# Softmax sums on GpSimd, attention's loads on the sync queue: an encoder block on one Trainium2 core

## The chip, the cores and the metric

The kernel runs on one core of a Trainium2 chip. A core has TensorE (PE, matmuls into PSUM), VectorE (DVE) and ScalarE (ACT), which read and write SBUF and PSUM, GpSimd (POOL), and the sync engine (SP), which here only issues transfers. Each engine works through its own instructions in order and waits on semaphores for the others. The metric is the device time of one execution in microseconds (us).

## The reference

One layer of a hybrid encoder on 2048 tokens of width 1024 and 16 meta tokens ahead of them. The input projection gives queries (4 heads of 128), keys and values (2 groups) and a Fourier part; attention and the Fourier part are normalized apart and projected back, then comes a feed-forward part of width 4096.

```python
proj = hn @ w_in[i]
q = axial_rope(rms_norm(q, g_q[i]), cos_r, sin_r, cos_c, sin_c)
k = axial_rope(rms_norm(k, g_k[i]), cos_r, sin_r, cos_c, sin_c)
attn = block_attention(q, k, v)
four = fourier_mix(u, w_fourier[i])
mixed = jnp.concatenate([rms_norm(attn, g_attn_out[i]), rms_norm(four, g_fourier_out[i])], axis=-1)
h = h + mixed @ w_out[i]
m = rms_norm(h, g_mlp[i])
h = h + jnp.square(jax.nn.relu(m @ w_up[i])) @ w_down[i]
...
s = jnp.einsum('bkgqd,bksd->bkgqs', qb, kt).astype(jnp.float32) * scale
p = jax.nn.softmax(s, axis=-1).astype(vt.dtype)
return jnp.einsum('bkgqs,bksd->bkgqd', p, vt)
```

## The kernel before

The kernel runs in stages: the input projection with norms and rotations (it stores queries, keys and values in DRAM, `q_d`, `k_d`, `v_n`, `v_m`); the U pass (`u_pass`), the Fourier transforms (`fourier`) and their output projection (`out_f`); attention's output projection (`out_a`); then up and down products of the feed-forward part. Most products are made of three matmuls of rounded parts (`mm3`, L81 to L83).

Attention (`attention`, L782) has no stage of its own. It is a generator of 16 units; a unit is 256 queries of one group of two heads (512 columns) against all keys, in 17 steps: 16 blocks of 128 keys and one of the meta tokens. `mix` (L1065) calls it so many steps for each step of the stage that it runs beside; the steps in the U pass, in the Fourier transforms, in `out_f` and in `out_a` are fixed by numbers (`ULEAD`, `FLEAD`, `OLEAD`, `STEPS_A`). So each engine's order is a weave of attention and the other stage. Where the code doesn't tie two instructions (`tc.issue_after`), a list scheduler chooses the order in which an engine's instructions stand.

`scores` (L812) makes one block's scores `s` on TensorE; ScalarE copies them to the pair's tile `S` (two blocks, 128 x 1024, L833), and VectorE keeps the running maximum `M` (L836, L839). `S` has 11 buffers (`S_BUFS`). At a unit's end `stats` (L859) turns the maximum into `mb` through TensorE, VectorE and ScalarE. `softmax` (L866) runs 17 + 3 steps behind the scores (`LEADT`): for each pair VectorE subtracts `mb` (L893), ScalarE takes the exponential in place (L894), VectorE adds the pair to `acc` (L898 for the first add, L900 for the other six), and TensorE multiplies by the values into `o` (L902). At the unit's end the two halves of `acc` are added (`sum`, L880), and `finish` (L904) divides.

Keys (`kt`, `load_k`), values (`vn`, `load_v`) and queries (`q`, `load_q`) are loaded on GpSimd's queue. GpSimd has little else in this part: the power -1/2 of each norm (`rstd_of`, L194: `rs_f` for the Fourier rows, `rs_a` and `rs_m` in `out_a`), sums of squares (L1018) and the loads of the Fourier tables (L608, L611). The sync queue loads and stores the rest, such as the residual rows `xo` (L1003) and `h_d`, and the attention output `o_d`.

Of the kernel before, what the change touches and what calls it, by code (L numbers as in the profile page):

```python
# [14 lines left out]
ALU = mybir.AluOpType  # L15
# [16 lines left out]
NT = SEQ // P  # L32
HALF = L // 2
QUART = HALF // 2
REM = 96
MR = 96
# [21 lines left out]
def f32v(ap):  # L58
    return ap.bitcast(F32)
# [26 lines left out]
def ins_of(x):  # L86
    return getattr(x, "ins", x)
# [49 lines left out]
def encoder_block(ctx: ExitStack, tc: tile.TileContext, x, meta, w_in, w_f,  # L137
                  w_out, w_up, w_down, g_fin, g_cols, g_rows, c_id, c_rope, c_dft, c_even, c_odd, c_rem, out):
    nc = tc.nc
# [21 lines left out]
    tp = Lines(tc.alloc_tile_pool(name="p1", bufs=2, side="right"), small)  # L161
# [20 lines left out]
    mhalf = const.tile([P, 8], F32, name="mhalf", tag="mhalf")  # L182
# [3 lines left out]
    c_ao = lambda k: cols[:, 16 + k:17 + k]  # L186
    c_fo = lambda k: cols[:, 20 + k:21 + k]

    def rstd_of(pool, ss, n, width, tag, rows=P):

        ms = pool.tile([P, n], F32, name="ms_" + tag, tag="ms_" + tag, bufs=2 if pool is tp else 4)
        nc.vector.tensor_scalar(ms[:rows], ss, 1.0 / width, EPS, op0=ALU.mult, op1=ALU.add)
        rs = pool.tile([P, n], F32, name="rs_" + tag, tag="rs_" + tag, bufs=2 if pool is tp else 4)
        nc.gpsimd.tensor_tensor(rs[:rows], ms[:rows], mhalf[:rows, :n], op=ALU.pow)  # L194
        return rs

    q_d = [dram.tile([P, 2, NQ, 256], F32, name=f"q_d{b}") for b in range(8)]
    k_d = dram.tile([P, NKV, 2, SEQ + MR], F32, name="k_d")
    v_n = dram.tile([P, NKV, NT, P], F32, name="v_n")
    v_m = dram.tile([MR, NKV, P], F32, name="v_m")  # L200
# [395 lines left out]
    def load_tables(tr):  # L596

        src, full, rest, n_tab = sources(tr)
        rem = ft.tile([P, NG, REM], F32, name=f"rem{tr}", tag="rem", bufs=1)
        nc.vector.memset(rem, 0.0)  # L600
        for o in (0, 32, 64):
            for lo, hi in rest:
                nc.vector.tensor_copy(rem[:, :, o:o + hi - lo], src[:, :, lo:hi])
                o += hi - lo
        tabs = []
        for nt in range(n_tab):
            t = ft.tile([P, 4, CHP], R32, name=f"tab{tr}_{nt}", tag="tab", bufs=T_BUFS)[:, :, :CH]
            nc.gpsimd.dma_start(t, c_even[tr, nt] if tr < 2 else c_odd[tr - 2, nt])  # L608
            tabs.append((t[:, 0:2], t[:, 2:4]))
        t = ft.tile([P, 2, CHP], R32, name=f"tabr{tr}", tag="tabr", bufs=2)[:, :, :CH]  # L610
        nc.gpsimd.dma_start(t[:REM], c_rem[tr])  # L611
        tabs.append(t)
        tables[tr] = tabs, rem

# [92 lines left out]
    def fourier():  # L707
        for par in range(2):
            pc = transform(2 * par)
            yield  # L710
            C = {}
            for g in range(NG):
                for c in range(2):
                    ps = pc(g, c)
                    C[g, c] = fp.pool.tile([P, CHP], F32, name=f"C{par}_{g}_{c}", tag="C", bufs=8)[:, :CH]
                    nc.scalar.copy(C[g, c], ps)
                yield
            sn = transform(2 * par + 1)
            yield
            for g in range(NG):  # L720
                for c in range(2):
                    ps = sn(g, c)
                    i0, step = (c * CH, 1) if par else (1 + c, 2)
                    m0 = -(min(i0 - 8, 0) // step)
                    e0, e1 = i0 + step * m0 - 8, i0 + step * (CH - 1) - 8
                    (t, col, _, n), = y_runs(par, e0, e1 + 1)
                    nc.vector.tensor_tensor(t[:, g, col:col + n:step], C[g, c][:, m0:], ps[:, m0:], op=ALU.subtract)
                    m1 = CH - 1 if (par == 0 and c == 1) else CH
                    e1 = SEQ // 2 - par - i0
                    e0 = e1 - step * (m1 - 1)  # L730
                    (t, col, _, n), = y_runs(par, e0, e1 + 1)
                    nc.vector.tensor_tensor(t[:, g, col:col + n:step][:, ::-1], C[g, c][:, :m1], ps[:, :m1], op=ALU.add)
                yield
# [14 lines left out]
    KC = 4 * P  # L748
    KCP = 640

    def load_k(u, g, c):
        n = KC + (MR if c == 3 else 0)
        kt = ap.tile([P, 2, KCP if c == 3 else KC], R32, name=f"kt_{u}_{c}", tag=f"KT{c // 3}", bufs=1 if c == 3 else 3)
        nc.gpsimd.dma_start(kt[:, :, :n], k_d[:, g, :, c * KC:c * KC + n])
        return kt

    def load_v(u, g, c):
        if c == 4:
            vt = ap.tile([P, P], R32, name=f"vm_{u}", tag="VM", bufs=1)
            nc.gpsimd.dma_start(vt[:MR], v_m[:, g])  # L760
        else:
            vt = ap.tile([P, 4, P], F32, name=f"vn_{u}_{c}", tag="VT", bufs=4)
            nc.gpsimd.dma_start(vt, v_n[:, g, 4 * c:4 * c + 4])
        return vt

    o_d = [dram.tile([P, 2, NQ, 512], F32, name=f"o_d{b}") for b in range(4)]
# [10 lines left out]
                    nc.sync.dma_start(f32v(A[:, e, k]), o_d[b][:, e, k])  # L777
        return AT[b]

    held = {}  # L780

    def attention():  # L782

        units = [(b0 + qh, g) for i, (b0, n) in enumerate(BLOCKS)
# [3 lines left out]
        def load_q(u):  # L788
            b, g = units[u]
            q = ap.tile([P, 2, 2, 256], R32, name=f"q_{u}", tag="q", bufs=2)  # L790
            nc.gpsimd.dma_start(q, q_d[b][:, :, 2 * g:2 * g + 2])
            return q.rearrange("p l h n -> p l (h n)")

        def start(u, q=None):
# [71 lines left out]
        def softmax(u, i):  # L866

            s = state[u]
            nm = f"{u}_{i}"
            vt = KV["v", u]  # L870
            if i == NT:
                S = s["S"][-1][:MR]
# [11 lines left out]
            j = i // 2  # L884
# [5 lines left out]
            p = S  # L890
            if i % 2 == 0:
                mb = s["mb"].rearrange("p (o n) -> p o n", o=1).broadcast_to([P, 2, 512])
                nc.vector.tensor_tensor(S, S, mb, op=ALU.subtract)  # L893
                held["exp"] = ins_of(nc.scalar.activation(p, S, AF.Exp, scale=ISQ))  # L894
                return
            v = vt[j // 2]
            if j == 1:
                nc.vector.tensor_tensor(acc, s["S"][0], p, op=ALU.add)  # L898
            elif j > 0:
                held["sub"] = ins_of(nc.vector.tensor_tensor(acc, acc, p, op=ALU.add))  # L900
            for e in range(2):
                nc.tensor.matmul(s["O"], v[:, 2 * j % 4 + e], p[:, e], start=i + e == 1, stop=False)  # L902

# [94 lines left out]
    def out_f():  # L998
# [6 lines left out]
        def rows(t):  # L1005

            hi = op_.tile([P, NG, P], R32, name=f"yh_{t}", tag="yh", bufs=2)
            lo = op_.tile([P, NG, P], R32, name=f"yl_{t}", tag="yl", bufs=2)
            sq = op_.tile([P, NG, P], F32, name=f"ysq_{t}", tag="ysq", bufs=2)
            for par in range(2):  # L1010
                for src, col, e, n in y_runs(par, 64 * t, 64 * t + 64):
                    y = src[:, :, col:col + n]
                    o = 2 * (e - 64 * t) + par
                    v = slice(o, o + 2 * n - 1, 2)
                    split(hi[:, :, v], lo[:, :, v], y)
                    nc.scalar.square(sq[:, :, v], y)
            for n in (2, 1):
                nc.gpsimd.tensor_tensor(sq[:, :n], sq[:, :n], sq[:, n:2 * n], op=ALU.add)  # L1018
            ops[t] = [hi, lo, sq]

        def scale(t):
# [820 lines left out]
```

## Time and profile before

| | us |
|---|---|
| runs, median (lowest to highest) | 2239.28 (2238.01 to 2241.07) |
| the profiled execution | 2236.94 |
| its span | 2235.2 |
| softmax adds on VectorE: L898, 16 of 1217 ns, and L900, 96 of 1219 ns | 19.5 and 117.0 |
| subtractions on VectorE, L893, 128 of 1222 ns | 153.0 |
| tensor instructions on GpSimd in attention's stages: sums of squares, L1018, 16 of 1293 ns and 16 of 1095 ns | 20.7 and 17.5 |

The profile is of one execution. Busy time is the time in which an engine worked on an instruction of the program; it says nothing on whether anything waited for it. Matmuls are pipelined, so that their rows overlap; the time from one start to the next is what one costs. A group's row gives the shape, the count, the busy time, the mean of one, and the idle time of the engine ahead of them with what ended it.

### The profile page before, as it was taken

The numbers are of one execution on the slowest core, as the hardware profiler recorded it, in microseconds if no ns is written. First come the engines' busy times: TensorE is split into PE (matmuls) and PEld (weight loads), VectorE is DVE, ScalarE is ACT, GpSimd is POOL, SyncE is SP. The second block draws the span as 40 slices with busy tenths as digits, with TensorE's granted clock in tenths as the row PEclk, the third lists the DMA queues.
The fourth block names the chain that finished last, engine by engine and source line by source line (L and its number), as shares of the span: only waits on it lengthen the run. The fifth ranks groups of instructions, "written<-read, shape, count | busy, mean of one in ns | idle before, by whom it ended". The sixth has DMA issues, their size and how long they took to land.

```text
span 2235.2 us, 27654 instructions
## 1 busy us (share of the span) xinstructions
PE 2219.0 (99%) x9890; PEld 1752.8 (78%) x9890; DVE 1681.4 (75%) x2260; ACT 1170.8 (52%) x1991; POOL 255.8 (11%) x301
## 2 busy tenths in 40 slices
PE   9999999999999999999999999999999999999998
PEld 7888867777777666677888888888888888888887
DVE  6566299999888989887676778679656555796795
ACT  6554255655554667677555654334455555443243
POOL 2223101012132212110000020000100000200000
PEclk9999999999999999999999999999999999999999
DMA  7685743345346434476767585434594434955442
GB/s 244 207 264 175 255 134 90 88 114 166 118 146 206 160 95 139 133 266 231 264 225 243 198 296 192 164 125 151 213 360 151 163 138 164 344 169 160 134 130 85
DMA packets 219914, 408.08 MB, mean 183 GB/s; under 512 B 19568, under 2 KB 97776, under 8 KB 218112
## 3 DMA queue, kind: packets, MB, share of 16 engines
q1 hardware_dynamic: 192000, 343.64, 45.9%
q0 software_dynamic: 27632, 62.41, 9.1%
q8 instruction: 78, 1.28, 0.2%
q14 instruction: 60, 0.49, 0.1%
q10 hardware_dynamic: 144, 0.26, 0.0%
HBM read 260.16 MB, written 146.08 MB: 182 GB/s over the span
## 4 chain that ended last, share of the span: by engine, by line
PE 45%; DVE 3%; DMA 3%; ACT 1%; issue 1%; SPq 0%; POOLq 0%; POOL 0%; DVEq 0%; ACTq 0%
PE dx L81 5%; PE dx L83 5%; PE dx L82 5%; PE dy L81 4%; PE dy L83 4%; PE dy L82 4%; PE ux L83 3%; PE ux L82 3%; PE ux L81 3%; PE uy L81 3%; PE uy L83 3%; PE uy L82 3%; DMA f_d<-lf 2%; DMA lf<-m_d 1%; DVE wul L72 1%
## 5 line engine op out<-in xcount | busy, mean ns | idle before, releaser
L71 ACT CAST ah<-a 128x1024 fp32r<-128x1024 f32 x108 | 113.0, 1050 | 263.7 <-PE dx L82 107.2
L902 PE MATMUL o<-S,vn 128*128 128x512 f32 x512 | 242.8, 595 | 0.0
L833 ACT COPY S<-s 128x512 f32<-128x512 f32 x256 | 147.8, 587 | 143.4 <-PE s L83 136.8
L83 PE MATMUL dx<-bh,al 128*128 128x512 f32 x496 | 192.5, 388 | 0.0
L82 PE MATMUL dx<-bl,ah 128*128 128x512 f32 x496 | 192.5, 388 | 0.0
L81 PE MATMUL dx<-bh,ah 128*128 128x512 f32 x496 | 192.5, 388 | 0.0
L83 PE MATMUL ux<-bf,wul 128*128 128x512 f32 x448 | 174.3, 389 | 0.7 <-DVE wul L72 0.7
L81 PE MATMUL ux<-bf,wuh 128*128 128x512 f32 x448 | 174.6, 390 | 0.0
L82 PE MATMUL ux<-bf,wuh 128*128 128x512 f32 x448 | 174.3, 389 | 0.0
L893 DVE TENSOR_TENSOR S<-S,mb 128x1024 f32<-128x1024 f32 x128 | 153.0, 1222 | 17.6 <-ACT mb L864 17.6
L894 ACT ACTIVATE S<-S 128x1024 f32<-128x1024 f32 x128 | 134.5, 1065 | 50.0 <-DVE S L893 48.8
L72 DVE TENSOR_TENSOR al<-a,ah 128x1024 fp32r<-128x1024 f32 x108 | 131.3, 1221 | 31.7 <-ACT ah L71 31.3
L81 PE MATMUL s<-q,kt 128*128 128x512 f32 (+1 forms) x272 | 151.0, 555 | 1.8 <-DMA kt<-k_d 1.0
L81 PE MATMUL dy<-bh,ah 128*128 128x512 f32 (+1 forms) x388 | 150.5, 388 | 0.0
L82 PE MATMUL dy<-bl,ah 128*128 128x512 f32 (+1 forms) x388 | 150.5, 388 | 0.0
L83 PE MATMUL dy<-bh,al 128*128 128x512 f32 (+1 forms) x388 | 150.5, 388 | 0.0
L902 PEld LDWEIGHTS o<-S,vn 128*128 128x128 f32 x512 | 93.3, 189 | 69.1 <-issue 58.5
L81 PE MATMUL uy<-bf,wuh 128*128 128x512 f32 x320 | 124.9, 390 | 1.2 <-ACT wuh L71 1.2
L82 PE MATMUL uy<-bf,wuh 128*128 128x512 f32 x320 | 124.8, 390 | 0.0
L83 PE MATMUL uy<-bf,wul 128*128 128x512 f32 x320 | 124.7, 390 | 0.0
L1306 ACT ACTIVATE c<-c 128x512 f32<-128x512 f32 x96 | 60.5, 631 | 121.4 <-DVE c L1354 117.8
L839 DVE TENSOR_TENSOR M<-M,S 128x1024 f32<-128x1024 f32 x96 | 117.8, 1227 | 7.3 <-ACT S L833 6.1
(330 smaller groups left out, 5576.5 us busy)
## 6 DMA issues: line engine op xcount, KB each, us to landing
a<-s_d SPq DMA_DIRECT2D x84, 512.0 KB, 3.8
R<-in_w_up_dram SPq DMA_DIRECT2D x32, 1024.0 KB, 5.5
s_d<-s SPq DMA_DIRECT2D x128, 256.0 KB, 2.1
s_d<-c SPq DMA_DIRECT2D x96, 256.0 KB, 2.7
d<-in_w_down_dram SPq DMA_DIRECT2D x48, 512.0 KB, 5.1
f_d<-lf SPq DMA_DIRECT2D x56, 256.0 KB, 3.1
bf<-f_d SPq DMA_DIRECT2D x7, 2048.0 KB, 13.8
hk<-ht_d SPq DMA_DIRECT2D x24, 512.0 KB, 4.8
```

What stands on the lines that cost most here:

```text
L71: self.high = nc.scalar.copy(hi, src)
L72: self.low = nc.vector.tensor_tensor(lo, src, f32v(hi), op=ALU.subtract)
L81: nc.tensor.matmul(out, a[0], b[0], start=first, stop=False, skip_group_check=chain)
L82: nc.tensor.matmul(out, a[0], b[1], start=False, stop=False, skip_group_check=chain)
L83: nc.tensor.matmul(out, a[1], b[0], start=False, stop=last, skip_group_check=chain)
L833: nc.scalar.copy(S[:, i % 2], ps)
L839: nc.vector.tensor_tensor(M, M, S, op=ALU.max)
L893: nc.vector.tensor_tensor(S, S, mb, op=ALU.subtract)
L894: held["exp"] = ins_of(nc.scalar.activation(p, S, AF.Exp, scale=ISQ))
L902: nc.tensor.matmul(s["O"], v[:, 2 * j % 4 + e], p[:, e], start=i + e == 1, stop=False)
L1306: nc.scalar.activation(dst, src, AF.Relu)
```

## The change

Six of a unit's seven adds to `acc` are issued on GpSimd; the last, with pair 7, stays on VectorE (now L908). A helper, `on_pool`, ties GpSimd's instructions from the adds, the norms of all but the first stage, the sums of squares, the Fourier tables and the meta values in program order. Keys, values and queries are loaded by the sync queue. The tables of transform 2 are loaded one step earlier, ahead of the products of transform 1.

```diff
+    held = {}
+
+    def on_pool(call, *args, **kw):
+
+        with tc.issue_after(held["pool"]) if "pool" in held else nullcontext():
+            held["pool"] = ins_of(call(*args, **kw))
...
-        nc.gpsimd.tensor_tensor(rs[:rows], ms[:rows], mhalf[:rows, :n], op=ALU.pow)
+        if pool is tp:
+            nc.gpsimd.tensor_tensor(rs[:rows], ms[:rows], mhalf[:rows, :n], op=ALU.pow)
+        else:
+            on_pool(nc.gpsimd.tensor_tensor, rs[:rows], ms[:rows], mhalf[:rows, :n], op=ALU.pow)
...
-            nc.gpsimd.dma_start(t, c_even[tr, nt] if tr < 2 else c_odd[tr - 2, nt])
+            on_pool(nc.gpsimd.dma_start, t, c_even[tr, nt] if tr < 2 else c_odd[tr - 2, nt])
...
             sn = transform(2 * par + 1)
+            if not par:
+                load_tables(2)
             yield
...
-        nc.gpsimd.dma_start(kt[:, :, :n], k_d[:, g, :, c * KC:c * KC + n])
+        nc.sync.dma_start(f32v(kt[:, :, :n]), k_d[:, g, :, c * KC:c * KC + n])
...
-            nc.gpsimd.dma_start(vt[:MR], v_m[:, g])
+            on_pool(nc.gpsimd.dma_start, vt[:MR], v_m[:, g])
...
-            nc.gpsimd.dma_start(vt, v_n[:, g, 4 * c:4 * c + 4])
+            nc.sync.dma_start(vt, v_n[:, g, 4 * c:4 * c + 4])
...
-            nc.gpsimd.dma_start(q, q_d[b][:, :, 2 * g:2 * g + 2])
+            nc.sync.dma_start(f32v(q), q_d[b][:, :, 2 * g:2 * g + 2])
...
-                nc.vector.tensor_tensor(S, S, mb, op=ALU.subtract)
+                held["sub"] = ins_of(nc.vector.tensor_tensor(S, S, mb, op=ALU.subtract))
...
-            if j == 1:
-                nc.vector.tensor_tensor(acc, s["S"][0], p, op=ALU.add)
+            if j == NT // 2 - 1:
+                nc.vector.tensor_tensor(acc, acc, p, op=ALU.add)
             elif j > 0:
-                held["sub"] = ins_of(nc.vector.tensor_tensor(acc, acc, p, op=ALU.add))
+                on_pool(nc.gpsimd.tensor_tensor, acc, s["S"][0] if j == 1 else acc, p, op=ALU.add)
...
-                nc.gpsimd.tensor_tensor(sq[:, :n], sq[:, :n], sq[:, n:2 * n], op=ALU.add)
+                on_pool(nc.gpsimd.tensor_tensor, sq[:, :n], sq[:, :n], sq[:, n:2 * n], op=ALU.add)
```

The orders below are those of the built programs; the lines of the changed kernel are 10 to 12 higher behind the helper. First VectorE at the start of a unit's softmax, in the first pass of `out_a`: `S_..` are pairs, `h` is the projection's add, `mx_l` the sum of the unit before.

```order
L893 TENSOR_TENSOR S_0_6503<-S_0_6503,mb_6924 128x1024
L893 TENSOR_TENSOR S_2_6557<-S_2_6557,mb_6924 128x1024
L893 TENSOR_TENSOR S_4_6614<-S_4_6614,mb_6924 128x1024
L893 TENSOR_TENSOR S_6_6655<-S_6_6655,mb_6924 128x1024
L1149 SCALAR_TENSOR_TENSOR h_1_6788<-poa_0_1_6961,rs_a,h_1_6788 128x512
L849 TENSOR_REDUCE mx_l_6989<-pm_l_6984 128x4
L898 TENSOR_TENSOR acc_6996<-S_0_6503,S_2_6557 128x1024
L912 RECIPROCAL rl_6991<-mx_l_6989 128x4
L836 TENSOR_TENSOR M_7005<-S_0_6922,S_2_6958 128x1024
L900 TENSOR_TENSOR acc_6996<-acc_6996,S_4_6614 128x1024
L839 TENSOR_TENSOR M_7005<-M_7005,S_4_7013 128x1024
L900 TENSOR_TENSOR acc_6996<-acc_6996,S_6_6655 128x1024
```

The same place in the changed kernel:

```order
L903 TENSOR_TENSOR S_0_6503<-S_0_6503,mb_6924 128x1024
L903 TENSOR_TENSOR S_2_6557<-S_2_6557,mb_6924 128x1024
L903 TENSOR_TENSOR S_4_6614<-S_4_6614,mb_6924 128x1024
L903 TENSOR_TENSOR S_6_6655<-S_6_6655,mb_6924 128x1024
L1159 SCALAR_TENSOR_TENSOR h_1_6788<-poa_0_1_6961,rs_a,h_1_6788 128x512
L859 TENSOR_REDUCE mx_l_6989<-pm_l_6984 128x4
L903 TENSOR_TENSOR S_8_6689<-S_8_6689,mb_6924 128x1024
L922 RECIPROCAL rl_6991<-mx_l_6989 128x4
L846 TENSOR_TENSOR M_7005<-S_0_6922,S_2_6958 128x1024
L903 TENSOR_TENSOR S_10_6722<-S_10_6722,mb_6924 128x1024
L849 TENSOR_TENSOR M_7005<-M_7005,S_4_7013 128x1024
L903 TENSOR_TENSOR S_12_6844<-S_12_6844,mb_6924 128x1024
```

The adds are gone from this stretch, and the subtractions of pairs 8 to 12 have moved up into their places. Next GpSimd at the same place, before the change:

```order
L194 TENSOR_TENSOR rs_a<-ms_a,mhalf 128x4
L763 DMA vn_2_6866<-v_n 128x512
L791 DMA q_7059<-q_d_111 128x2x512
L194 TENSOR_TENSOR rs_m<-ms_m,mhalf 128x1
L763 DMA vn_3_6934<-v_n 128x512
L760 DMA vm_6950<-v_m 96x128
L194 TENSOR_TENSOR rs_m<-ms_m,mhalf 128x1
```

And in the changed kernel, where L194 is the line of `on_pool`:

```order
L194 TENSOR_TENSOR rs_a<-ms_a,mhalf 128x4
L194 TENSOR_TENSOR acc_6597<-acc_6597,S_8_6283 128x1024
L194 TENSOR_TENSOR acc_6597<-acc_6597,S_10_6326 128x1024
L194 TENSOR_TENSOR acc_6597<-acc_6597,S_12_6367 128x1024
L194 DMA vm_6950<-v_m 96x128
L194 TENSOR_TENSOR rs_m<-ms_m,mhalf 128x1
L194 TENSOR_TENSOR acc_6996<-S_0_6503,S_2_6557 128x1024
L194 TENSOR_TENSOR acc_6996<-acc_6996,S_4_6614 128x1024
L194 TENSOR_TENSOR acc_6996<-acc_6996,S_6_6655 128x1024
L194 TENSOR_TENSOR acc_6996<-acc_6996,S_8_6689 128x1024
L194 TENSOR_TENSOR rs_m<-ms_m,mhalf 128x1
```

The norms' powers stand between the adds, up to four of which are ahead of one `rs_m`. Last the sync queue beside `out_f`, before the change (`h_d` and `o_d` are stores, `l_d` and `rb` a unit's sums on their way through DRAM):

```order
L1050 DMA h_d_124<-xo_5965 128x1024
L1003 DMA xo_6169<-in_x_dram 128x1024
L914 DMA l_d_2810<-rl_6151 128x4
L1050 DMA h_d_125<-xo_6064 128x1024
L916 DMA rb_6154<-l_d_2810 128x512
L1003 DMA xo_6252<-in_x_dram 128x1024
L935 DMA o_d_2800<-ohl_6404 128x2x256
```

In the changed kernel the loads of keys for the next group stand between them:

```order
L1060 DMA h_d_124<-xo_5965 128x1024
L1013 DMA xo_6169<-in_x_dram 128x1024
L766 DMA kt_0_6167<-k_d 128x2x512
L924 DMA l_d_2810<-rl_6151 128x4
L1060 DMA h_d_125<-xo_6064 128x1024
L926 DMA rb_6154<-l_d_2810 128x512
L1013 DMA xo_6252<-in_x_dram 128x1024
L945 DMA o_d_2800<-ohl_6404 128x2x256
L766 DMA kt_1_6250<-k_d 128x2x512
```

A wait of `kt_0` for its buffer now has the store and the load of the rows behind it.

More of the change, by code (lines that the diff above doesn't have):

```diff
@@ L607, in load_tables @@
             t = ft.tile([P, 4, CHP], R32, name=f"tab{tr}_{nt}", tag="tab", bufs=T_BUFS)[:, :, :CH]
-            nc.gpsimd.dma_start(t, c_even[tr, nt] if tr < 2 else c_odd[tr - 2, nt])
+            on_pool(nc.gpsimd.dma_start, t, c_even[tr, nt] if tr < 2 else c_odd[tr - 2, nt])
             tabs.append((t[:, 0:2], t[:, 2:4]))
         t = ft.tile([P, 2, CHP], R32, name=f"tabr{tr}", tag="tabr", bufs=2)[:, :, :CH]
-        nc.gpsimd.dma_start(t[:REM], c_rem[tr])
+        on_pool(nc.gpsimd.dma_start, t[:REM], c_rem[tr])
         tabs.append(t)
@@ L778, in a_operand @@
         return AT[b]
-    held = {}
     def attention():
```

## The prediction, made before the run

> **What bounds the kernel now.** I read the page's busy shares first, then the windows of the three attention stages, then the spacing of the matmuls, because a busy TensorE need not be one at its peak.
>
> ```profile
> PE 2219.0 (99%) x9890; PEld 1752.8 (78%) x9890; DVE 1681.4 (75%) x2260; ACT 1170.8 (52%) x1991; POOL 255.8 (11%) x301
> ```
>
> The change touches only the time in which attention runs. The windows below (window, TensorE busy and count, weight loads, VectorE, ScalarE, GpSimd, clock, DMA) cut it into stage A (U pass beside attention), B (Fourier and its output projection beside it) and C (attention's output projection beside it); the last row is the feed-forward part.
>
> ```profile
> 300.00:400.00 100.00, 100.00 (x391) 69.79 (x390) 95.10 (x137) 56.38 (x92) 11.42 (x17) 1.00 0.45 111
> 400.00:750.00 350.00, 348.15 (x1600) 256.48 (x1600) 312.06 (x432) 194.40 (x343) 75.36 (x82) 1.00 0.46 144
> 750.00:950.00 200.00, 199.35 (x781) 134.71 (x780) 181.50 (x219) 132.56 (x213) 41.98 (x25) 1.00 0.38 118
> 1050.00:2200.00 1150.00, 1149.16 (x5066) 950.05 (x5065) 827.83 (x990) 548.50 (x754) 44.43 (x76) 1.00 0.58 197
> ```
>
> VectorE is 95, 89 and 91% busy in A, B and C, against 72% later. So it looks like a second bound there. Is it the first? The timeline of TensorE gives what one matmul costs from start to start.
>
> ```profile
> 642.00 1.88 PE L902 MATMUL o<-S,vn 128*128 128x512 f32 x4
> 643.32 0.80 PE L81 MATMUL s<-q,kt 128*96 128x512 f32 x1
> 643.95 0.39 PE L82 MATMUL s<-q,kt 128*96 128x512 f32 x1
> 644.18 0.39 PE L83 MATMUL s<-q,kt 128*96 128x512 f32 x1
> 1012.37 1.03 PE L1173 MATMUL pmt<-ident,h 128*128 128x128 f32 x8
> ```
>
> A score matmul follows the one before it by 0.23 us (643.95 to 644.18). The four `o` records therefore fill 642.00 to 643.72, 0.43 each; a transpose takes at most 0.13. Now the groups of stage C:
>
> ```profile
> L902 PE MATMUL o<-S,vn 128*128 128x512 f32 x173 | 81.9, 594 | 0.0
> L81 PE MATMUL s<-q,kt 128*128 128x512 f32 x79 | 44.5, 563 | 0.0
> L81 PE MATMUL poa<-woh,at 128*128 128x512 f32 x73 | 29.7, 407 | 0.0
> L1173 PE MATMUL pmt<-ident,h 128*128 128x128 f32 x44 | 6.7, 272 | 0.0
> ```
>
> 173 x 0.43 = 74 us; scores and projection, three lines each, 3 x (79 + 73) x 0.227 = 103 us; the 44 transposes and the 108 small products that the window's count of 781 leaves, at 0.11 to 0.13, make 17 to 20. That is 194 to 197 of 200 us: **TensorE is the bound even where VectorE is 91% busy**, and a faster VectorE can win 3 to 6 us in 200, at most some 16 in the 650 us of the three stages. In 1050 to 2200 nothing changes.
>
> **The change part by part.** Each of the 16 units sums 8 pairs of exponentials in 7 adds; 6 adds leave VectorE, the last stays. As many adds per unit carry line L900 now, so its counts give the number moved in each stage: 17 in A, 43 in B, 31 in C.
>
> ```profile
> L900 DVE TENSOR_TENSOR acc<-acc,S 128x1024 f32<-128x1024 f32 x17 | 20.7, 1218 | 0.0
> L900 DVE TENSOR_TENSOR acc<-acc,S 128x1024 f32<-128x1024 f32 x43 | 52.5, 1220 | 0.0
> L900 DVE TENSOR_TENSOR acc<-acc,S 128x1024 f32<-128x1024 f32 x31 | 37.8, 1218 | 0.0
> ```
>
> GpSimd's adds on the same kind of operands are the squares of L1018; the fastest of 32, a 128x128, took 459 ns (min/median/max in the second row), an undisturbed 128x256 took 0.73 us:
>
> ```profile
> 569.85 0.73 POOL L1018 TENSOR_TENSOR ysq<-ysq 128x256 f32<-128x256 f32 x1 [9.97 <-ACT ysq L1016]
> L1018 POOL TENSOR_TENSOR ysq<-ysq x32: 459/794/5774, 535.4 to 697.6; 128x256 f32<-128x256 f32 x16, 128x128 f32<-128x128 f32 x16
> ```
>
> That is (0.73 - 0.46)/128 = 2.1 ns an element. An add of 1024 is then 0.73 + 768 x 0.0021 = 2.36 us, an estimate. Six take 14.2 us of a unit; in C a unit lasts 200/(31/6) = 38.7 us. As work of its own, GpSimd has room. The Trainium skill, GPSIMD Engine Reference, section 3.1, gives 4497 ns for 2048 elements, an estimate of 2.25 us here; by it each add would block 0.11 us less, and the first term of the sum below would be 12 instead of 22 us.
>
> But the two engines do not work side by side. The longest of those 32 adds is in this stretch of the timeline, GpSimd's row first:
>
> ```profile
> 660.47 11.31 POOL L1018 TENSOR_TENSOR ysq<-ysq 128x256 f32<-128x256 f32 x2
> 661.03 1.22 DVE L900 TENSOR_TENSOR acc<-acc,S 128x1024 f32<-128x1024 f32 x1
> 662.17 1.22 DVE L893 TENSOR_TENSOR S<-S,mb 128x1024 f32<-128x1024 f32 x1
> 663.30 1.22 DVE L839 TENSOR_TENSOR M<-M,S 128x1024 f32<-128x1024 f32 x1
> 664.44 1.22 DVE L900 TENSOR_TENSOR acc<-acc,S 128x1024 f32<-128x1024 f32 x1
> 665.58 0.74 DVE L1046 SCALAR_TENSOR_TENSOR xo<-pof,rs_f,xo 128x512 f32<-128x512 f32 x1
> ```
>
> Two adds worth 1.2 us needed 11.3. While VectorE runs instructions with two operands in SBUF back to back, GpSimd gets nothing; the 128x256 add ends only in the 0.74 us of L1046, whose one operand (`pof`) is in PSUM. The other way round, VectorE waits:
>
> ```profile
> 674.90 1.13 DVE L944 TENSOR_TENSOR sq<-sq,O 128x256 f32<-128x256 f32 x1 [0.28 <-ACT O L937]
> 675.02 1.34 POOL L1018 TENSOR_TENSOR ysq<-ysq 128x256 f32<-128x256 f32 x2
> L944 DVE TENSOR_TENSOR sq<-sq,O 128x256 f32<-128x256 f32 x4 | 1.7, 418 | 0.0
> ```
>
> L944 took 1.13 us instead of 0.42: the 0.71 more is the GpSimd add that began at 675.02. The Trainium skill, SBUF — State Buffer, section "Who interferes with whom", states this as a rule: a VectorE instruction with two SBUF inputs and a GpSimd one that reads SBUF exclude each other for the whole instruction. The trace agrees in both directions. By the rule alone, with no add under other work, the sum would be its upper end below.
>
> So a moved add frees 1.14 us of VectorE (661.03 to 662.17) and blocks it for b. Begun at the start of a PSUM-operand instruction it blocks 2.36 - 0.74 = 1.62 us; with nothing to lie under, 2.36; wholly in a gap of VectorE, 0. I take 1.62, since L1046 shows that start, and keep both ends. VectorE's need in a stage is its busy time - 1.14 n + n b:
> - A: 95.1 - 19.4 + 17b = 103.3 (115.8 at b = 2.36), in 100 us.
> - B: 312.1 - 49.0 + 43b = 332.7 (364.6), in 350 us.
> - C: 181.5 - 35.3 + 31b = 196.4 (219.4), in 200 us.
>
> To this come waits that the adds cannot fill: at a unit's seam VectorE waits for the new maximum and its broadcast, when the old unit's adds are done; in B also for the projection. Rows for A, B and C:
>
> ```profile
> L893 DVE TENSOR_TENSOR S<-S,mb 128x1024 f32<-128x1024 f32 x19 | 22.7, 1219 | 2.1 <-ACT mb L864 2.1
> L849 DVE TENSOR_REDUCE mx_m<-pm_m 128x4 f32<-128x512 f32 x2 | 1.4, 688 | 1.9 <-PE pm_m L847 1.9
> L893 DVE TENSOR_TENSOR S<-S,mb 128x1024 f32<-128x1024 f32 x56 | 67.3, 1226 | 7.8 <-ACT mb L864 7.8
> L849 DVE TENSOR_REDUCE mx_m<-pm_m 128x4 f32<-128x512 f32 x7 | 4.8, 689 | 3.1 <-PE pm_m L847 3.0
> L1046 DVE SCALAR_TENSOR_TENSOR xo<-pof,rs_f,xo 128x512 f32<-128x512 f32 x32 | 23.8, 743 | 12.8 <-PE pof L83 9.0 <-issue 3.3 <-POOL rs_f L194 0.5
> L893 DVE TENSOR_TENSOR S<-S,mb 128x1024 f32<-128x1024 f32 x44 | 52.4, 1218 | 7.7 <-ACT mb L864 7.7
> L849 DVE TENSOR_REDUCE mx_m<-pm_m 128x4 f32<-128x512 f32 x6 | 4.1, 690 | 4.0 <-PE pm_m L847 3.9
> ```
>
> With 4.0, 23.7 and 11.7 us of them, A needs 107.3 (+7.3), B 356.4 (+6.4), C 208.1 (+8.1): **+22 us**. At b = 2.36 without these waits A, B, C give +15.8, +14.6, +19.4, together +50.
>
> A second term: a pair's tile is free for new scores only when its add is done. There are 11; scores run 17 + 3 steps ahead, 20 x 8/17 = 9.4 pairs, so one is spare, 2 of 17 steps, 4.6 us of the 38.7. An add that starves like the one above (5.1 us, 660.47 to 665.58) ends 7.5 us after its exponential, 2.9 us too late; ScalarE's copy of the scores stands, then TensorE. From none to one in every unit (0 to 46 us); I take one in four units, 4 x 2.9 = **+12 us**, the low side, since the median of the 32 adds of squares, 794 ns, is near the undisturbed time.
>
> The tied order on GpSimd: `rs_f`, `rs_a` and `rs_m` now stand behind some adds, and the projection's add waits for the first two. I cost this at 0, as the matmuls of the next tile cover it; without that cover it is at most 2 x 2.36 us for each of the 4 `rs_a`, 19 us. The earlier tables of transform 2: 0, hidden under the products of transform 1; at most one VectorE copy set of below 1 us.
>
> The moved loads: GpSimd waited for TensorE in front of them, and nobody stood behind it.
>
> ```profile
> POOL vn L763 <- PE o L902: 126.5, 15, 18.4
> POOL kt L754 <- PE s L83: 112.1, 12, 21.8
> ```
>
> Those waits now stand on the sync queue, with the residual tiles `xo` and the stores behind them. Since a load is placed about where its buffer comes free, I take 0; the upper end is in the rivals. Below zero, a load that starts earlier wins nothing: TensorE waited for `kt` hardly at all, as its floor above shows.
>
> Sum on the profiled execution (2236.9 us, its span 2235.2): 2236.9 + 22 + 12 = 2271; the runs' median 2239.3 is 2.4 above it, so **2273 us**.
>
> **The rivals.**
> - *The adds fall into VectorE's gaps* (not slower). It decides where b stays below 1.14. For it: A to C have 61 us of VectorE idle, and 104 more after the move, against 91 x 2.36 = 215 us. Then VectorE is relieved and TensorE gains 5 to 16 us: 2223 to 2234. Against it: gaps shorter than an add. 0.15.
> - *Nothing moves*: b between 1.14 and 1.4, TensorE stays the bound: 2235 to 2243. 0.10.
> - *Full exclusion and frequent starving*: +50 and a late add in every second unit (+23): 2312, from 2295 to 2335. The order below speaks for it: the subtractions of a unit now stand in runs of four, which leave GpSimd no opening. 0.11.
> - *The sync queue blocks*: if a quarter of kt's 112 us reaches TensorE through a late `xo`, +28: 2267, alone, from 2255 to 2290. For it: waits up to 21.8 us; against: they are short in the order's own place. 0.05.
>
> **How the numbers follow.** Forecast 0.59 (2250 to 2295); with the last two rivals slower has 0.75. 0.2%, 4.5 us, is about what a measurement can tell; within it 0.10, faster 0.15. The range leaves out the better half of the faster case (0.09) and the worst of full exclusion (0.06): 2230 to 2312.
>
> **What would show it.** Right: GpSimd adds of about 2.4 us with a long tail, VectorE subtractions well over 1.22 us where they overlap them, TensorE's o and s spacing above 0.43 and 0.23 in A and C, ScalarE's score copies waiting for an add, stages A to C longer by 34 us and the rest unchanged. Wrong: subtractions at 1.22 us beside running adds, or attention ending at the same time with VectorE idler. A later `xo` with a sync queue waiting for `kt` would speak for the fourth rival.

## The result, and the profile after

The changed kernel takes **2382.91 us** in the median (2381.93 to 2383.12) beside 2238.65 us (2237.34 to 2241.07) for the one before in the same runs: ratio 1.0642, 95% interval 1.0624 to 1.0661. It is 144 us slower; 34 were forecast, and the range ended at 2312.

First the page's busy line of the changed kernel, its clock row and the first groups that changed (busy time, mean ns of one, idle time ahead of them):

```profile
span 2379.8 us, 27746 instructions
PE 2261.0 (95%) x9890; PEld 1771.8 (74%) x9890; DVE 1729.6 (73%) x2164; ACT 1168.3 (49%) x1991; POOL 472.1 (20%) x341
PEclk9999999989999899989999999999999999999999
L194 POOL TENSOR_TENSOR acc<-acc,S 128x1024 f32<-128x1024 f32 x80 | 236.9, 2962 | 15.5 <-ACT S L904 11.6
L903 DVE TENSOR_TENSOR S<-S,mb 128x1024 f32<-128x1024 f32 x128 | 211.4, 1687 | 24.3 <-ACT mb L874 24.3
```

96 adds of 1.22 us (117 us) have left VectorE, and yet it is busy for 48 us more than before (1681.4): a subtraction takes 1687 ns in the mean where it took 1222. Where is the time? The windows show attention, from the first score matmul to the last product with the values, and the feed-forward part behind it; first before the change, then after (window, busy time of TensorE, weight loads, VectorE, ScalarE, GpSimd, then clock and DMA):

```profile
253.30:967.30 714.00, 710.07 (x3016) 504.73 (x3014) 625.81 (x827) 417.91 (x700) 135.61 (x134) 1.00 0.44 134
1013.80:2235.20 1221.40, 1213.53 (x5361) 1003.65 (x5359) 875.88 (x1066) 590.71 (x829) 48.84 (x84) 1.00 0.57 195
```

```profile
255.70:1107.70 852.00, 745.29 (x2999) 518.02 (x2999) 673.56 (x730) 414.45 (x698) 355.14 (x177) 0.94 0.36 111
1158.60:2379.80 1221.20, 1213.53 (x5360) 1003.97 (x5358) 875.73 (x1066) 590.84 (x829) 48.73 (x84) 1.00 0.57 195
```

The feed-forward part is unchanged; attention has grown by 138 us. In it TensorE went from 4 to 107 us of idle time, and its busy time from 710 to 745 us, at a granted clock of 0.94 instead of 1.00: 103 and 35 us make up the 138. And VectorE isn't short of time on the whole: it is idle for 178 of 852 us, 88 of 714 before. Who let TensorE wait? The wait of TensorE for score copies before, then the waits of TensorE and ScalarE in the changed kernel (total us, times, longest):

```profile
PE s L81 <- ACT S L833: 0.8, 1, 0.8
```

```profile
PE s L81 <- ACT S L843: 64.0, 24, 8.1
PE pm_m L857 <- DVE M L838: 19.7, 7, 9.2
ACT S L904 <- DVE S L903: 81.2, 48, 6.7
ACT S L843 <- POOL acc L194: 19.3, 6, 8.4
```

TensorE waits for ScalarE's score copies, whose PSUM bank it needs. The timeline of one unit shows why they are late: some lines of GpSimd, VectorE, ScalarE and TensorE from 845 to 864 us.

```profile
845.43 9.88 POOL L194 TENSOR_TENSOR acc<-acc,S 128x1024 f32<-128x1024 f32 x3
846.45 3.30 DVE L846 TENSOR_TENSOR M<-S,S 128x1024 f32<-128x1024 f32 x1
849.67 3.41 DVE L903 TENSOR_TENSOR S<-S,mb 128x1024 f32<-128x1024 f32 x1
853.00 3.38 DVE L849 TENSOR_TENSOR M<-M,S 128x1024 f32<-128x1024 f32 x1
853.11 1.06 ACT L904 ACTIVATE S<-S 128x1024 f32<-128x1024 f32 x1 [3.58 <-DVE S L903]
857.55 2.19 ACT L904 ACTIVATE S<-S 128x1024 f32<-128x1024 f32 x2 [2.42 <-DVE S L903]
860.49 0.63 ACT L1134 ACTIVATE hj<-h 128x512 f32<-128x512 f32 x1 [0.74 <-DVE h L1159]
861.68 0.63 ACT L884 ACTIVATE S<-S 96x512 f32<-96x512 f32 x1
862.22 1.05 ACT L843 COPY S<-s 128x512 f32<-128x512 f32 x2
862.84 0.79 PE L81 MATMUL s<-q,kt 128*128 128x512 f32 x1 [4.77 <-ACT S L843]
863.43 0.63 PE L82 MATMUL s<-q,kt 128*128 128x512 f32 x1
863.86 0.63 PE L83 MATMUL s<-q,kt 128*128 128x512 f32 x1
```

GpSimd and VectorE alternate here: for each add of 3.3 us VectorE gets one instruction done, in 3.4 us instead of 1.2. Over the whole run the 47 subtractions that had an add beside them took 2488 ns in the mean, the other 81 took 1222. ScalarE stands 3.58 and 2.42 us in front of exponentials whose subtraction is late. The score copy has nothing to do with those, but it stands behind them in ScalarE's order, and behind work of the projection (`hj`, 0.74 us of wait) and of a unit's end, and runs at 862.22. TensorE, in order too, sits idle for 4.77 us, and then its clock is halved: a score matmul comes 0.43 us after the last (863.43 to 863.86), where 0.23 was usual.

### The profile page after: what moved, and what is told of

Its sections match the earlier page's. It is cut to its first block, busy times and chain, and to the rows that moved or that the text cites. A ratio compares the mean times of both kernels' runs of the same rounds, so it can differ in the third digit from the quotient of the medians.

```text
span 2379.8 us, 27746 instructions
## 1 busy us (share of the span) xinstructions
PE 2261.0 (95%) x9890; PEld 1771.8 (74%) x9890; DVE 1729.6 (73%) x2164; ACT 1168.3 (49%) x1991; POOL 472.1 (20%) x341
## 4 chain that ended last, share of the span: by engine, by line
PE 66%; DVE 16%; issue 5%; DMA 4%; POOL 4%; ACT 4%; SPq 1%; POOLq 0%; DVEq 0%; ACTq 0%
PE dx L82 5%; PE dx L81 5%; PE dx L83 5%; DVE S L903 4%; PE o L912 4%; PE dy L81 4%; PE dy L82 4%; PE dy L83 4%; PE ux L83 4%; PE ux L81 4%; PE ux L82 3%; POOL acc L194 3%; PE uy L81 3%; PE uy L82 3%; PE uy L83 3%
## 5 line engine op out<-in xcount | busy, mean ns | idle before, releaser
L912 PE MATMUL o<-S,vn 128*128 128x512 f32 x512 | 255.0, 620 | 0.0
L194 POOL TENSOR_TENSOR acc<-acc,S 128x1024 f32<-128x1024 f32 x80 | 236.9, 2962 | 15.5 <-ACT S L904 11.6
L903 DVE TENSOR_TENSOR S<-S,mb 128x1024 f32<-128x1024 f32 x128 | 211.4, 1687 | 24.3 <-ACT mb L874 24.3
L849 DVE TENSOR_TENSOR M<-M,S 128x1024 f32<-128x1024 f32 x96 | 148.1, 1543 | 39.3 <-ACT S L843 38.2
L912 PEld LDWEIGHTS o<-S,vn 128*128 128x128 f32 x512 | 98.7, 200 | 72.9 <-issue 60.8
L81 PEld LDWEIGHTS s<-q,kt 128*128 128x128 f32 (+1 forms) x272 | 53.2, 196 | 112.6 <-ACT S L843 86.8
L1438 POOL DMA_DIRECT2D d<-in_w_down_dram x16 | 11.6, 729 | 593.4 <-PE ux L83 289.0
L81 PE MATMUL uy<-bf,wuh 128*128 128x512 f32 x320 | 124.9, 390 | 1.2 <-ACT wuh L71 1.2
```

The lines of the kernel that those rows point to most:

```text
L81: nc.tensor.matmul(out, a[0], b[0], start=first, stop=False, skip_group_check=chain)
L194: held["pool"] = ins_of(call(*args, **kw))
L849: nc.vector.tensor_tensor(M, M, S, op=ALU.max)
L903: held["sub"] = ins_of(nc.vector.tensor_tensor(S, S, mb, op=ALU.subtract))
L1438: eng.dma_start(r, w_down[r0:r0 + 256, (j - 1) * 512:j * 512].rearrange("(p r) d -> r p d", r=P))
```

## The experiments

All ratios are to the kernel before, run beside it, with a 95% interval. In a code cut `...` stands for lines left out. **Blocked time**, where it is given, is the time of VectorE's instructions above the lower quartile of their line and shape, less the 11 to 18 us of it that the kernels without adds on GpSimd show too; for the changed kernel that is 149 us, 1.55 us for each of 96 adds.

### Which part of the change costs the time

The adds back on VectorE, all else of the change kept:

```diff
-                on_pool(nc.gpsimd.tensor_tensor, acc, s["S"][0] if j == 1 else acc, p, op=ALU.add)
+                nc.vector.tensor_tensor(acc, s["S"][0] if j == 1 else acc, p, op=ALU.add)
```

> The changed kernel, but its six adds stand on VectorE again; the tied GpSimd order, the loads on the sync queue and the early tables are kept. If the adds on GpSimd cost the 144 us (theory PORT: GpSimd and VectorE exclude each other while both have operands in SBUF, and the delays pass down the in-order engines), this is back at the kernel before: 2230 to 2250 us. If the tied order or the sync queue costs them (theory QUEUES), it stays above 2300. In between, the distance to 2238 us is the share of the queues; I expect at most 10 us of it.

2239.63 us, ratio 1.0008 (0.9998 to 1.0018). The tied order, the loads on the sync queue and the early tables cost nothing that can be measured, together. Then the adds alone, in the kernel before (the last add stays on VectorE):

```diff
...
-                held["sub"] = ins_of(nc.vector.tensor_tensor(acc, acc, p, op=ALU.add))
+                nc.gpsimd.tensor_tensor(acc, s["S"][0] if j == 1 else acc, p, op=ALU.add)
```

> The kernel before with one edit: the six adds on GpSimd, not tied to anything; keys, values, queries and tables are loaded on GpSimd's queue as before. PORT: the whole loss or more, 2360 to 2420 us, VectorE's subtractions at 1.6 us or more in the mean. QUEUES: within 20 us of 2238.

2400.72 us, 1.0723 (1.0707 to 1.0739): 163 us lost, more than by the whole change. And the whole change without the ties:

```diff
-        with tc.issue_after(held["pool"]) if "pool" in held else nullcontext():
-            held["pool"] = ins_of(call(*args, **kw))
+        call(*args, **kw)
```

> The changed kernel without the ties of GpSimd's program order; the adds stay on GpSimd and the loads on the sync queue. If the ties cost much (adds wait behind a norm's power whose input is not there yet: 112 us of waits at rs_m, 90 at rs_f in the changed kernel), it is faster by 30 us or more, below 2350. If PORT is nearly all, it stays within 15 us of 2383, and may be slower, since a scheduler's order can put loads and powers behind adds.

2397.98 us, 1.0714 (1.0698 to 1.073). With the adds on GpSimd the ties are worth 15 us; the waits at the norms' powers, which I had suspected, are no cost to be won back by dropping the ties. Last the adds left out altogether, so that VectorE has its relief and the changed order, and GpSimd reads nothing:

```diff
...
             if j == NT // 2 - 1:
-                nc.vector.tensor_tensor(acc, acc, p, op=ALU.add)
-            elif j > 0:
-                on_pool(nc.gpsimd.tensor_tensor, acc, s["S"][0] if j == 1 else acc, p, op=ALU.add)
+                nc.vector.tensor_tensor(acc, s["S"][0], p, op=ALU.add)
```

> The changed kernel with the six adds left out altogether (pairs 1 to 6 are missing from the sums; a constant is added at the unit's end so that no sum is zero). VectorE is relieved as in the change, and its subtractions and ScalarE's exponentials stand in the changed order, but GpSimd reads nothing. PORT: at or below the kernel before, by the prediction's floor of TensorE no lower than 2222 us: 2222 to 2240. If the new order of VectorE and ScalarE (subtractions and exponentials ahead of score copies) is itself the cost (theory ORDER), it stays above 2280.

2237.96 us, 1.0002 (0.9992 to 1.0011). Two things follow: the new order of subtractions and exponentials is no cost by itself, and taking 117 us of work off VectorE gains nothing that can be measured. So the change had next to nothing to win.

### Is it the read of SBUF that blocks?

A GpSimd write in the place of the add, to the pair's tile when TensorE has read it:

```diff
...
+            if 0 < j < NT // 2 - 1:
+                on_pool(nc.gpsimd.memset, p, 0.0)
```

> The changed kernel with each of the six adds replaced by a GpSimd memset of the pair's tile, after TensorE has read it (the sums of pairs 1 to 6 are left out, a constant is added to the sum at the unit's end). GpSimd has the same number of instructions in the same tied order and holds the pair's tile at least as long, but reads nothing in SBUF. PORT: VectorE's subtractions stay at 1.22 us and the time at 2235 to 2250. If the late release of the tiles or the wait of in-order GpSimd counts for itself (theory RELEASE): above 2270 with subtractions undisturbed.

2234.55 us, 0.9984 (0.9975 to 0.9994). Once more for its profile:

> The kernel of write_only once more, for a profile: GpSimd writes the pair's tile and reads nothing. PORT: 96 memsets of about 0.95 us beside subtractions of 1.22 us, the time at 2235; if a write alone excluded VectorE's instructions, subtractions above 1.3 us in the mean.

2233.76 us in one run, and these groups:

```profile
L194 POOL MEMSET S<- 128x1024 f32 x96 | 91.6, 955 | 442.0 <-PE o L910 417.5 <-ACT S L904 9.3 <-ACT hj L1134 4.9
L903 DVE TENSOR_TENSOR S<-S,mb 128x1024 f32<-128x1024 f32 x128 | 152.4, 1227 | 22.4 <-ACT mb L874 22.3
```

96 writes leave the subtractions at 1227 ns. In this run 12 subtractions and 39 maxima `M` had a write beside them, and took 1219 and 1223 ns in the mean. The tiles that they hold longer, and a GpSimd that waits for TensorE for 417 us, cost nothing here. Now a copy of the pair to `acc`, which reads one operand where the add reads two:

```diff
...
-                on_pool(nc.gpsimd.tensor_tensor, acc, s["S"][0] if j == 1 else acc, p, op=ALU.add)
+                on_pool(nc.gpsimd.tensor_copy, acc, p)
```

> The changed kernel with a GpSimd copy of the pair to acc in place of each of the six adds (one input in SBUF instead of two; the sums of pairs 1 to 5 are left out, a constant is added at the unit's end). If any GpSimd instruction that reads SBUF excludes VectorE's, subtractions that overlap a copy take longer than 1.22 us by up to the copy's duration, and the time lies between 2250 and 2383 in proportion to that duration (half the add's: about 2310). If only GpSimd instructions with two inputs exclude: 2235 to 2245 and subtractions at 1.22 us.

2268.2 us, 1.0136 (1.0121 to 1.0151): 31 us lost. The copies' durations (min, median, max, first and last start), and the group of the subtractions:

```profile
L194 POOL COPY acc<-S x96: 1027/1625/8405, 295.9 to 989.4; 128x1024 f32<-128x1024 f32 x96
```

```profile
L903 DVE TENSOR_TENSOR S<-S,mb 128x1024 f32<-128x1024 f32 x128 | 174.3, 1397 | 22.5 <-ACT mb L874 22.5
```

The fastest copy takes 1027 ns, the fastest add 2358; blocked time goes down to 50 us, but not to nothing. The 49 subtractions that had a copy beside them took 1681 ns in the mean, the other 79 took 1221. One operand is enough to block. On VectorE's side I took the second SBUF operand away from the running maximum, which now reads the scores in PSUM:

```diff
...
-                nc.vector.tensor_tensor(M, M, S, op=ALU.max)
...
+                nc.vector.tensor_tensor(M[:, i % 2], M[:, i % 2], ps, op=ALU.max)
```

> The changed kernel with the running maximum M taken from the scores in PSUM, two halves of 512 a pair, instead of from the pair's copy in SBUF: 128 x 1024 maxima with two operands in SBUF become twice as many 128 x 512 ones with one in SBUF and one in PSUM. If the exclusion holds only for instructions with two operands in SBUF, the M instructions stay undisturbed beside GpSimd's adds (about 0.7 us each, by the 0.74 us of L1046), the subtractions stay disturbed, and part of the loss goes: 2300 to 2360. If every VectorE instruction waits for GpSimd, the M instructions reach 2 us and the time stays at 2380 or above.

> The same edit of M in the kernel before, adds on VectorE: the control. VectorE has 16 x 7 x about 0.25 us more to do; TensorE stays the bound: 2235 to 2250. A maximum that holds a PSUM bank until VectorE has read it could cost more: up to 2270.

2364.19 us, 1.0566 (1.0549 to 1.0584), and 2244.73 us, 1.0035 (1.0022 to 1.0048), for the control: 119 us between them. Of the first, with GpSimd's adds in it, the group of the subtractions, and the durations of the maxima:

```profile
L904 DVE TENSOR_TENSOR S<-S,mb 128x1024 f32<-128x1024 f32 x128 | 213.6, 1692 | 22.1 <-ACT mb L875 22.1
```

```profile
L850 DVE TENSOR_TENSOR M<-M,s x192: 622/681/690, 259.5 to 1055.6; 128x512 f32<-128x512 f32 x192
```

Not one of 192 maxima with a PSUM operand took over 690 ns, and 47 of them had an add beside them; the subtractions, two operands in SBUF, are as slow as in the changed kernel. The exclusion is as the prediction had it. But with a good part of VectorE's instructions out of it the loss is still 119 us, and the time 4 us above what I expected.

### How the loss goes with the blocked time

Half the adds on GpSimd (the unit's first three), then all of them in two halves of 512 columns:

```diff
-            if j == NT // 2 - 1:
+            if j > 3:
```

> The changed kernel with only the first three adds of a unit on GpSimd; the other four stand on VectorE. Theory NEED (a stage takes what VectorE needs in its mean, the prediction's formula): half the adds give needs of 103, 347 and 201 us in stages of 100, 350 and 200, so about +4 us: 2240 to 2247. Theory BURST (an add blocks VectorE in the first 20 us behind a unit's maximum, in which VectorE has no idle time, and the idle time later in the unit can't be used): each blocked microsecond there is lost, half the adds cost about half of 144: 2290 to 2330.

2321.92 us, 1.0376 (1.0361 to 1.0392). Not the 4 us of the prediction's formula: half the adds cost more than half of the loss, as BURST had it.

```diff
-                on_pool(nc.gpsimd.tensor_tensor, acc, s["S"][0] if j == 1 else acc, p, op=ALU.add)
+                for h in range(2):
+                    on_pool(nc.gpsimd.tensor_tensor, acc[:, h], (s["S"][0] if j == 1 else acc)[:, h], p[:, h], op=ALU.add)
```

> The changed kernel with each add on GpSimd in two halves of 512 columns. Blocked time in all is about the same, but one VectorE instruction waits for a half at most (1.3 instead of 2.4 us) and VectorE gets a turn between the halves, while each add lasts over more of VectorE's instructions. BURST: if VectorE's pace in the first 20 us is what counts, 2340 to 2380, a small gain; if the adds' own lateness counts (the pairs' tiles come free later, theory RELEASE), above 2390.

2370.73 us, 1.0596 (1.058 to 1.0612): 12 us better than whole adds. Then subtractions tied behind the newest maximum and exponentials behind the newest score copy, with a control on the kernel before:

```diff
...
-                held["sub"] = ins_of(nc.vector.tensor_tensor(S, S, mb, op=ALU.subtract))
+                with tc.issue_after(held["max"]):
+                    held["sub"] = ins_of(nc.vector.tensor_tensor(S, S, mb, op=ALU.subtract))
...
```

> The changed kernel with the order of the code kept on two engines: each subtraction stands behind the newest maximum M on VectorE, each exponential behind the newest score copy on ScalarE, so that they alternate and no run of subtractions stands ahead of M or of a copy. The adds stay on GpSimd and block as long (1.5 us each). BURST: blocked time is spread over the unit and M is no longer late, so a good part of 144 us goes: 2270 to 2330. If what counts is the blocked time alone (NEED with a larger b, or a straight sum of 96 x 1.5): 2370 to 2400, no gain.

> The same two ties in the kernel before, adds on VectorE: the control of the run above. TensorE stays the bound, I expect 2235 to 2260; the adds on GpSimd then cost the difference of the two runs, by BURST clearly less than 144 us.

2367.03 us, 1.0574 (1.0558 to 1.059), against 2262.42 us, 1.0111 (1.0096 to 1.0126): the order costs 25 us by itself, and in it the adds on GpSimd cost 105. Of the changed kernel's time only 16 us go, not the 53 to 113 that BURST gave. Blocked and lost time side by side:

| kernel | blocked, us | lost, us |
|---|---|---|
| the changed kernel | 149 | 144 |
| adds alone, untied | 187 | 163 |
| first three adds | 63 | 84 |
| halves | 122 | 133 |
| copies in place of adds | 50 | 31 |
| maxima from PSUM, to its control | 117 | 119 |
| order of the code, to its control | 163 | 105 |

Blocked time costs 0.6 to 1.3 times its length, though VectorE, summed over attention, has room for it: 88 us of idle time in the kernel before, and 110 that six adds a unit free (96 x 1.14, by the prediction's count), 55 for the first three. Why isn't it absorbed?

### The same time on VectorE itself

No adds, but two instructions of 1.22 and 0.43 us more on VectorE for each of the six pairs, ahead of the exponential; and the adds on VectorE, with 0.4 us more behind each:

```diff
...
+                    nc.vector.tensor_tensor(S, S, S, op=ALU.max)
+                    held["pad"] = ins_of(nc.vector.tensor_tensor(S[:, 0, :256], S[:, 0, :256], S[:, 0, :256], op=ALU.max))
...
```

> Neither engine adds (the sums of pairs 1 to 6 are left out, a constant is added at the unit's end); instead each of the six pairs costs VectorE two instructions more, 128 x 1024 and 128 x 256, about 1.14 + 0.4 = 1.55 us, tied between the pair's subtraction and the next one, ahead of the exponential. This puts the blocked time of the changed kernel on VectorE itself, at the place where it falls, with no GpSimd in it. VectorE's mean need is that of the kernel before plus 0.4 us an add, 40 us. If VectorE's time at that place is worth its full length (theory PLACE, a sharper BURST), 2340 to 2390; if only the mean need counts (NEED), 2240 to 2265, and the loss of the changed kernel has something more in it, that the order was made without knowing of the blocked time.

> The six adds on VectorE, each followed by a 128 x 256 instruction of about 0.4 us on acc: the same 1.55 us for each pair, at the place of the adds, behind the exponential, where nothing but the unit's sum waits. NEED and PLACE both say little here: 2240 to 2260. If it loses more than 40 us, VectorE's time counts wherever it stands, and the place decides nothing.

2261.58 us, 1.0105 (1.009 to 1.012), and 2254.81 us, 1.0073 (1.0056 to 1.009): 24 and 17 us. So VectorE can take that time, at either place, nearly as the prediction's formula has it, which gives 15 us for b = 1.55 and 25 for 1.65. My expectation that the place decides fell.

What these two have and the changed kernel doesn't is an order that was made with that time in it. So I built the kernel without adds once, took the order of TensorE, VectorE and ScalarE from it, and imposed it on the kernel with the additional instructions, each behind its subtraction (`order` has the places from the first build, `row` an engine's instructions, `of` the additional ones of a subtraction):

```python
nc, _, names = build(inputs, False, None)
nc, arrays, _ = build(inputs, True, orders(nc.m.functions[0].blocks, names))
...
for n in order[e]:
    for i in (row[n], *of.get(row[n].name, ())):
        if last is not None:
            edge(i, last)
        last = i
```

> The work of pad_early (no adds, 1.55 us more of VectorE behind the subtraction of each of the pairs 1 to 6), but TensorE, VectorE and ScalarE keep the order that the scheduler made for the kernel without adds and without the longer time (no_adds); the additional instructions are put behind their subtractions in it. Theory ORDER-BLIND (the loss is large since the order of the engines is made without knowing of the blocked time): as much lost as with the adds on GpSimd, 2330 to 2390. Theory GPSIMD (its blocking itself is worse than the same time on VectorE: it comes in bursts, and the adds end late): about as pad_early, 2255 to 2275.

2382.81 us, 1.0651 (1.0635 to 1.0667). That is a loss of the changed kernel's size, with no add and no blocking in it: the same work as the run of 2261.58 us, in an order that doesn't know of it. (That the two times agree to 0.1 us is chance: the additional instructions are 159 us of work, the changed kernel's blocked time is 149.) In the traces TensorE, VectorE, ScalarE and GpSimd keep the order of the kernel without adds, instruction for instruction, with the additional ones between; on the sync queue 48 of 973 places differ, and TensorE waited for loads in this part for 0.8 us. So the additional instructions in that order make the loss. Its profile has the same signature, first the windows of attention in the kernel without adds and in this one, then TensorE's longest waits, then the subtractions (undisturbed) and the additional instructions:

```profile
256.00:966.30 710.30, 707.54 (x3000) 502.22 (x3000) 525.27 (x732) 415.75 (x700) 74.56 (x82) 1.00 0.42 134
255.90:1102.40 846.50, 751.12 (x3000) 519.49 (x3000) 681.05 (x922) 417.40 (x698) 67.56 (x81) 0.95 0.35 112
```

```profile
PE s L81 <- ACT S L843: 60.2, 26, 9.4
```

```profile
L904 DVE TENSOR_TENSOR S<-S,mb 128x1024 f32<-128x1024 f32 x128 | 155.9, 1226 | 21.5 <-ACT mb L874 21.5
L906 DVE TENSOR_TENSOR S<-S 128x1024 f32<-128x1024 f32 x96 | 117.6, 1225 | 3.3
L907 DVE TENSOR_TENSOR S<-S 128x256 f32<-128x256 f32 x96 | 41.2, 429 | 3.3
```

Without the additional instructions VectorE is idle for 185 of 710 us, and yet with 159 us more attention takes 846 us, TensorE waits for score copies for 60 us (64 in the changed kernel), and the clock falls to 0.95. The other way round: the adds on GpSimd, in the order that was made with the additional instructions, which are then left away. They stand ahead of the exponential in the first of these runs, and behind it, where an add can begin, in the second:

> The changed kernel, adds on GpSimd, with the order of TensorE, VectorE and ScalarE that the scheduler makes when VectorE has 1.55 us more to do behind the subtraction of each of the pairs 1 to 6; this additional work is not in the program itself. ORDER-BLIND: most of the loss goes, 2255 to 2300. GPSIMD: 2340 to 2390.

> As adds_known, but the order of the three engines is made with the 1.55 us (here four instructions of 0.42 us) behind the exponential of each of the pairs 1 to 6, where GpSimd's add can begin, and not behind the subtraction. If ORDER-BLIND is all and adds_known missed only the place of the blocked time: below 2300. If knowing a mean place isn't enough, because what GpSimd blocks shifts from unit to unit: 2330 to 2383.

2346.67 us, 1.0487 (1.047 to 1.0505), and 2361.06 us, 1.0548 (1.0531 to 1.0566). The waits for score copies have gone to 9.2 us in the first (in the second they are 49.9), but others are there:

```profile
PE pm_m L857 <- DVE M L838: 20.7, 8, 4.7
PE o L917 <- ACT S L909: 13.8, 10, 3.1
PE s L81 <- ACT S L843: 9.2, 6, 2.8
```

36 and 22 us come back, not the 83 to 128 that ORDER-BLIND gave: both times fall in the ranges of its rivals, by which GpSimd's blocking is worse than the same time on VectorE (GPSIMD), or shifts from unit to unit. VectorE is blocked for about 154 and 171 us in them, no less than in the changed kernel. An order made for a mean place of the blocked time doesn't absorb it. So the order without that time in it is enough to lose 145 us, but it isn't shown to be all that the adds lose by.

## Why the size was wrong

- **TensorE is the bound, little to win.** Right, and sharper than forecast: I gave up to 16 us, and leaving the adds out wins none that can be measured.
- **A GpSimd add takes 2.36 us; each blocks VectorE for 1.62.** The add is right: the fastest took 2358 ns. For the blocked time, 149 us over 96 adds is 1.55, but that it comes so close is partly luck. I reasoned from an add that begins beside an instruction with an operand in PSUM; in the trace, by the measure above, 57 of the 96 adds block VectorE for 2.0 to 2.5 us, 19 for less than 0.2 and the rest lie between, and 1.55 is the mean of that mix.
- **"VectorE's need in a stage is its busy time - 1.14 n + n b": +22 us.** This is the step that failed. It lets freed time stand against blocked time, and lets VectorE's idle time take the rest. That holds if the order of the engines is made for it: with the time on VectorE and in the plan, the runs lost 24 and 17 us. It fails for time that the order doesn't have in it: the same time out of the plan lost 145. The three engines' instructions were placed for an undisturbed VectorE, subtractions moved up into the places of the adds; when one is late, score copies and other engines' work behind it wait although they are ready, and TensorE, which had 4 us to spare in attention, stands. Freed time counts for nothing there, and blocked time for about its whole length: 149 us blocked, 144 lost. That these two are so close is chance too, since the other kernels lost 0.6 to 1.3 times what was blocked. For the adds on GpSimd the account is in part argued, as the last two runs show.
- **Late pair tiles: one unit in four, +12 us.** ScalarE's copies waited for an add 6 times, 19.3 us in all; the term had 4 waits and 12 us, so it was somewhat low. What of it reached TensorE wasn't measured apart; writes that held the tiles longer cost nothing.
- **Ties at 0, at most 19 us lost.** 0 without adds on GpSimd, and 15 us gained with them.
- **Moved loads and tables at 0.** Right (1.0008), and with it the rival of the sync queue fell.
- **The rivals.** Adds in VectorE's gaps and no change at all: wrong by the subtractions' mean of 1687 ns. Full exclusion with frequent starving, 2295 to 2335, came nearest, 48 us short, but it too counted need against capacity.
- **The clock** wasn't in the forecast. In the changed kernel's trace attention has 16 stretches at a granted clock of 0.5, about 100 of its 852 us together, which is the mean of 0.94. TensorE stood for part of that time, and its busy time rose by 35 us. The kernel before has none there.

Open is why an order that reckons with about 1.65 us a pair brings so little back with the adds on GpSimd. In the timeline above three instructions in a row are each held for over 2 us, and 19 of the 96 adds hold next to nothing, where the plan has the same time for each pair; that this is the reason was not tried.

## What to carry to other kernels

Before work is moved to take load off an engine, leave it out altogether in one run: here that wins nothing, so a better place for the adds had next to nothing to win. Where an engine that sets the end is fed by others in a fixed order, count time that this order doesn't know of at about its full length (0.6 to 1.3 times here), and give no credit for idle or freed time elsewhere. GpSimd beside a busy VectorE makes such time, as soon as it reads SBUF and VectorE's instructions have two operands there.

## What the runs showed of the hardware

- GpSimd's claim on VectorE goes by operands, on both sides: a write of 955 ns blocks none of the subtractions and maxima with two operands in SBUF, a copy that reads one operand does, and none of the maxima with one operand in PSUM was held. VectorE's copies from SBUF to SBUF are a case of their own. Two of 8 columns, 0.16 us in the median of their line, took 2.30 and 2.35 us beside an add, while those of 4 columns stayed at 0.15; and one of 20 columns, 0.17 us otherwise, took 1.03 us beside a write. The line in the changed kernel:

```profile
L613 DVE COPY rem<-UA x9: 151/160/2349, 454.9 to 534.2; 128x8 f32<-128x8 f32 x3, 128x4 f32<-128x4 f32 x3, 128x20 f32<-128x20 f32 x3
```

- Of TensorE's stops of 3 us or more in the changed kernel, all but one were followed, 2.0 to 4.9 us from their start, by a granted clock of 0.5 for 3.4 to 10.2 us; the other fell in such a stretch. Of its four stops of 2.1 to 2.8 us, two were followed by it too and two were not. In this window of 10 us, which has most of the stop of the timeline above, the mean is 0.66:

```profile
858.45:868.45 10.00, 5.61 (x11) 3.38 (x12) 9.18 (x10) 6.21 (x12) 5.79 (x3) 0.66 0.29 105
```
